# Low half of the expert gates built by ScalarE one token at a time, and the experts' split activations moved in memory

## The chip, the cores and the metric

The kernel runs on one core of a Trainium2 chip. The metric is the time of one execution on the device in microseconds (us), the median of several executions. The engines named below are TensorE (PE, with its weight loads as PEld), VectorE (DVE), ScalarE (ACT), GpSimd (POOL) and SyncE (SP), whose queue issues the DMAs.

## The reference, cut to what matters

Two blocks of two layers each run over 256 tokens of width 1024. The change lies in the expert part of the first block, which runs once in each of its two layers:

```python
N_KEYS, N_EXPERTS, PEER_HEADS, PEER_TOPK = 128, 128 * 128, 8, 16

def peer(xn, w_q, sub_keys, u, v):
    q = (xt @ w_q).astype(float32).reshape(t, PEER_HEADS, 2, PEER_HALF)
    sc = einsum('thpc,pnc->thpn', q, sub_keys)
    top_s, top_i = lax.top_k(sc, PEER_TOPK)
    cand = top_s[:, :, 0, :, None] + top_s[:, :, 1, None, :]
    best_s, best_c = lax.top_k(cand.reshape(t, PEER_HEADS, 256), PEER_TOPK)
    expert = i1 * N_KEYS + i2
    gate = softmax(best_s, axis=-1)
    ...
    act = gelu(einsum('cd,chkd->chk', xc, u[ec]))
    return einsum('chk,chkd->cd', gc * act, v[ec])
```

So each token has 128 pairs of expert and gate, and the result is the sum over those experts of gate times gelu(x·u) times v.

## The kernel before, in words

The kernel computes all 16384 experts densely. `act` holds 128 x 128 x 256 values: for expert 128 n + p the partition is p, the second index n, the third the token. In each layer `peer` goes through three stages.

**Routing** finds the 128 experts and gates of each token, while the first products with u already run (`u_whole`, line 888: one block is 256 experts, two transposes of `raw` into `ut` on VectorE and 16 float32 products of 256 columns on TensorE, which the trace records as 32). At its end `mT`, `nT` and `gp` hold, by partition for the 128 pairs and by column for the 256 tokens, the expert's two indices and the gate, scaled by 32768 and split into a high and a low fp16 half (lines 839 and 840).

**The sweep** (`spread_gates`, line 848) turns this list into a dense gate for every expert. It takes GT = 4 tokens at a time, 64 groups in a layer. For a group VectorE makes `oh` (line 859, where mT equals the index), `eq` (line 861, where nT equals the index) and `rhs` (line 863, eq times the high and the low half of gp, 2 x 128 x 4 values). TensorE multiplies `oh` with `rhs` token by token, high and low half into the same bank of PSUM (line 868, eight products of 128 columns, each with its own weight load). VectorE then multiplies the experts already computed by their gates (line 872) and ScalarE stores the gates of the others (line 874). `oh` has two buffers, `eq` one, `rhs` four. Between the groups stand the blocks of u; after every block come four groups (`SWEEP_STEPS`), and `u_out` (lines 924 to 927) applies gelu and, where gates are there, the gate.

**The v stage** (`v_pair`, line 930) multiplies the 16384 gated values with v. `ah` and `al` are the high and low parts of two slices of `act`; they live in the buffers of `rhs`, and are the stationary operands of 24 products of 512 columns in each of 64 pairs (line 943), so 3072 in two layers. The moving operands are the split rows of v in the ring of weights (`whi`, `wlo`). The last 27 blocks of u run between these pairs with the split scheme (`u_split`, lines 198 to 200 and 906 to 910).

A scheduler puts the instructions of each engine into one fixed order by priorities; `K.ahead()` draws the loads and splits of weights forward, and the products of the gates have a priority of their own (`GPRIO`). Each engine works through its order and waits in place. `raw`, into which the DMAs write, has three buffers.

**Places in memory.** `K.shift` puts an unused tile of so many bytes ahead of a pool's next tiles. In the built program the ring's `whi` and `wlo` begin at multiples of 512 bytes (51200, 55296, 59392, 63488, 67584, 71680). `rhs`, and so `ah` and `al`, begin at 213056, which is 64 bytes past a multiple of 512. The tiles `x`, moving operands of lines 198 to 200, begin 64 bytes below a multiple of 512.

## Time and profile before

| | us |
|---|---|
| median of 3 runs | 3620.2 (3617.34 to 3631.05) |
| profiled execution, its own time | 3630.35 |
| profiled execution, span of its instructions | 3628.6 |
| first sweep, from the first to the last product of gates | 608.6 to 783.9 |
| second sweep | 1926.8 to 2103.6 |
| v stages with the last blocks of u | 783.9 to 1340 and 2103.6 to 2640 |

The granted clock of TensorE over the whole span was 0.975. Busy shares are means over stages with different limits, so the sweep has to be looked at by itself: how long each engine is busy in it, where TensorE stops, and what ends each stop.

### The profile page before, as it was taken

How to read it: one execution, taken by the hardware profiler on the slowest of the kernel's cores; microseconds unless marked ns; L12 is line 12 of the kernel's file. 1: busy time of each engine (PE TensorE's matmuls, PEld its weight loads, DVE VectorE, ACT ScalarE, POOL GpSimd, SP SyncE). 2: the span in 40 equal slices, each digit the busy share in tenths (PEclk: the TensorE clock that was granted, in tenths of full speed). 3: DMA queues.
4: the chain of work that ended last, by engine and by line, in shares of the span. 5: the costliest groups of instructions: out<-in, count | busy, mean ns of one | idle time of the engine just before them, and what ended most of it. 6: DMA issues, size and time to landing. Idle time of an engine off the chain costs nothing. (4 is left out here: it accounts for less than half of the span.)

```text
span 3628.6 us, 60192 instructions
## 1 busy us (share of the span) xinstructions
PE 3484.8 (96%) x23381; PEld 3187.9 (88%) x23381; DVE 2623.3 (72%) x4704; ACT 1475.1 (41%) x2418; POOL 604.2 (17%) x583
## 2 busy tenths in 40 slices
PE   8999998999999999999999999999989999999999
PEld 8898887888888889998888888888789899988999
DVE  6967668876666568775668866666578877698775
ACT  6455111234444446553112144444445344444434
POOL 1200111000000012101120000000033543345441
PEclk9999999999999999999999999999989999999999
DMA  7775756436666567765765346665666534665433
GB/s 178 180 187 140 164 128 139 93 94 189 184 184 187 196 156 173 196 159 147 155 138 113 94 130 190 188 189 186 190 151 141 109 85 116 164 129 120 96 85 126
DMA packets 433976, 541.70 MB, mean 149 GB/s; under 512 B 28665, under 2 KB 392219, under 8 KB 432667
## 3 DMA queue, kind: packets, MB, share of 16 engines
q1 hardware_dynamic: 433690, 537.86, 58.5%
q8 instruction: 183, 3.00, 0.4%
q14 instruction: 103, 0.84, 0.1%
HBM read 530.39 MB, written 6.32 MB: 148 GB/s over the span
## 5 line engine op out<-in xcount | busy, mean ns | idle before, releaser
L170 DVE TENSOR_TENSOR wlo<-raw,whi 128x1024 fp32r<-128x1024 f32 x670 | 862.7, 1293 | 325.8 <-ACT whi L167 311.3
L167 ACT ACTIVATE whi<-raw 128x1024 fp32r<-128x1024 f32 x696 | 728.7, 1051 | 709.0 <-PE mm L199 271.9
L898 PE MATMUL mm<-x,ut 128*128 128x256 f32 x2368 | 542.6, 386 | 1.2 <-ACT act L927 1.2
L200 PE MATMUL mm<-x,wlo 128*128 128x256 f32 x1760 | 506.6, 288 | 14.4 <-DVE wlo L170 14.1
L898 PEld LDWEIGHTS mm<-x,ut 128*128 128x128 f32 x2368 | 453.0, 194 | 64.3 <-ACT act L927 3.9
L198 PE MATMUL mm<-x,whi 128*128 128x256 f32 x1760 | 504.4, 287 | 3.3 <-ACT whi L167 3.3
L199 PE MATMUL mm<-x,whi 128*128 128x256 f32 x1708 | 488.9, 286 | 0.0
L200 PE MATMUL gg<-x,wlo 128*128 128x256 f32 (+1 forms) x1456 | 410.5, 282 | 9.3 <-DVE wlo L170 9.1
L198 PE MATMUL gg<-x,whi 128*128 128x256 f32 (+1 forms) x1456 | 410.9, 282 | 4.9 <-ACT whi L167 4.9
L199 PE MATMUL gg<-x,whi 128*128 128x256 f32 x1400 | 393.6, 281 | 1.3 <-DVE x L303 1.3
L200 PEld LDWEIGHTS mm<-x,wlo 128*128 128x128 f32 x1760 | 340.8, 194 | 18.2 <-DVE wlo L170 17.2
L198 PEld LDWEIGHTS mm<-x,whi 128*128 128x128 f32 x1760 | 340.7, 194 | 10.7 <-issue 5.6
L199 PEld LDWEIGHTS mm<-x,whi 128*128 128x128 f32 x1708 | 331.6, 194 | 1.9 <-issue 0.7
L943 PE MATMUL ax<-wlo,ah 128*128 128x512 f32 x1024 | 323.0, 396 | 2.6 <-DVE wlo L170 2.6
L943 PE MATMUL ax<-whi,al 128*128 128x512 f32 x1024 | 321.4, 395 | 0.0
L200 PEld LDWEIGHTS gg<-x,wlo 128*128 128x128 f32 (+1 forms) x1456 | 276.3, 190 | 11.7 <-DVE wlo L170 11.3
L943 PE MATMUL ax<-whi,ah 128*128 128x512 f32 x1024 | 286.6, 395 | 0.0
L198 PEld LDWEIGHTS gg<-x,whi 128*128 128x128 f32 (+1 forms) x1456 | 275.7, 189 | 8.2 <-ACT whi L167 5.6
L894 DVE STREAM_TRANSPOSE ut<-raw 128x1024 f32<-128x1024 f32 x148 | 181.9, 1236 | 130.8 <-DMA raw<-in_peer_u_dram 114.1
L199 PEld LDWEIGHTS gg<-x,whi 128*128 128x128 f32 x1400 | 265.9, 190 | 3.5 <-DVE x L303 1.4
L943 PEld LDWEIGHTS ax<-wlo,ah 128*128 128x128 f32 x1024 | 190.2, 187 | 54.8 <-DVE wlo L170 9.2
L943 PEld LDWEIGHTS ax<-whi,al 128*128 128x128 f32 x1024 | 191.7, 187 | 47.1
(534 smaller groups left out, 6593.5 us busy)
## 6 DMA issues: line engine op xcount, KB each, us to landing
raw<-in_w_in_dram SPq DMA_DIRECT2D x592, 256.0 KB
raw<-in_peer_u_dram SPq DMA_DIRECT2D x512, 256.0 KB
raw<-in_peer_v_dram SPq DMA_DIRECT2D x128, 1024.0 KB
raw<-in_w_branch_dram SPq DMA_DIRECT2D x16, 1024.0 KB
raw<-in_w_out_dram SPq DMA_DIRECT2D x16, 1024.0 KB
raw<-in_w_peer_q_dram SPq DMA_DIRECT2D x64, 256.0 KB
raw<-in_w_in_dram SPq DMA_DIRECT2D x64, 128.0 KB
raw<-in_w_branch_dram SPq DMA_DIRECT2D x32, 256.0 KB
```

The source lines that it names most:

```text
L167: nc.scalar.activation(view(hi), src, AF.Copy)
L170: (nc.gpsimd if pool else nc.vector).tensor_tensor(view(lo), src, view(hi).bitcast(F32), ALU.subtract)
L198: t.matmul(out, wh, xh, start=start, stop=False)
L199: t.matmul(out, wh, xl, start=False, stop=False)
L200: t.matmul(out, wl, xh, start=False, stop=stop)
L894: nc.vector.transpose(turned[jh], blk)
L898: nc.tensor.matmul(ps[:, jh], turned[jh][:, k].rearrange("p j c -> p (j c)"), xs[:, k], start=k + jh == 0, stop=k == KT - 1 and jh == 1)
L943: nc.tensor.matmul(out[tb][c], lhs[:, j, ts], r[:, c * 512:c * 512 + 512], start=b + j == 0 and lhs is ah and r is vh, stop=b == 63 and j ...
```

## The change

It does three things.

1. `rhs` is made by two engines. VectorE multiplies eq with the high half alone (512 values instead of 1024). The low half is kept in float32 (`gl`), and ScalarE makes its part of `rhs` with four activations a group, one for each token, 128 values each: it reads the token's column of eq, every fourth value, scales it by the column of `gl`, one value for each partition, and writes one run of 128 values.
2. The products of line 868 stand in two lines, 871 (high) and 872 (low); the low one now reads its moving operand as one run and not every fourth value.
3. `SHIFTS["peer"]` goes from 64 to 0 bytes in both layers. `gp` shrinks by 512 bytes and `gl` adds 1024, so that `rhs`, `ah` and `al` begin at 213504 instead of 213056 in the built program: a multiple of 512 bytes, as the ring's tiles do.

```diff
--- before.py
+++ after.py
@@ -33,7 +33,7 @@
 
 
 URGENT = 3000
-SHIFTS = {"zp": (0, 288), "zp2": (384, 384), "ple": (384, 128), "peer": (64, 64)}
+SHIFTS = {"zp": (0, 288), "zp2": (384, 384), "ple": (384, 128), "peer": (0, 0)}
 SQ_ACT = (2, 5, 7)
 HPOOL = ()
 WPOOL = 0
@@ -73,6 +73,7 @@
         self.consts()
 
     def shift(self, pool, size, name="shift"):
+
 
         if size:
             pool.tile([128, size // 4], F32, name=name, bufs=1)
@@ -719,7 +720,8 @@
     nc.vector.tensor_copy(io4, io[:, :, None].to_broadcast([128, 128, GT]))
     mT = pool.tile([128, S], FP16, name="mT")
     nT = pool.tile([128, S], FP16, name="nT")
-    gp = pool.tile([128, 2, S], FP16, name="gp")
+    gp = pool.tile([128, S], FP16, name="gp")
+    gl = pool.tile([128, S], F32, name="gl")
     sc_b = [scratch([128, 4, 128]) for _ in range(2)]
     qs_b = [scratch([128, 2, S]) for _ in range(2)]
     cand_b = [scratch([128, 2, NCAND]) for _ in range(2)]
@@ -836,9 +838,8 @@
                 nc.scalar.activation(dst, ps[:, 0:S], AF.Copy)
             else:
                 rest = m_f.rearrange("p b n -> p (b n)")
-                nc.scalar.activation(gp[:, 0], ps[:, 0:S], AF.Copy, scale=GSCALE)
-                nc.vector.scalar_tensor_tensor(gp[:, 1], ps[:, 0:S], GSCALE, gp[:, 0], op0=ALU.mult,
-                                               op1=ALU.subtract)
+                nc.scalar.activation(gp, ps[:, 0:S], AF.Copy, scale=GSCALE)
+                nc.vector.scalar_tensor_tensor(gl, ps[:, 0:S], GSCALE, gp, op0=ALU.mult, op1=ALU.subtract)
             yield
 
     made, spread = [0], [0]
@@ -859,14 +860,16 @@
             nc.vector.tensor_tensor(oh, io4, tok(mT), ALU.is_equal)
             eq = pool.tile([128, 128, GT], FP16, name="eq", tag="eq", bufs=1)
             nc.vector.tensor_tensor(eq, io4, tok(nT), ALU.is_equal)
-            rhs = pool.tile([128, 2, 128, GT], FP16, name="rhs", tag="rhs", bufs=4)
-            nc.vector.tensor_tensor(rhs, eq[:, None].to_broadcast([128, 2, 128, GT]),
-                                    gp[:, :, None, ts].to_broadcast([128, 2, 128, GT]), ALU.mult)
+            rhs = pool.tile([128, 2, 128 * GT], FP16, name="rhs", tag="rhs", bufs=4)
+            hi = rhs[:, 0].rearrange("p (n t) -> p n t", t=GT)
+            lo = rhs[:, 1].rearrange("p (t n) -> p t n", t=GT)
+            nc.vector.tensor_tensor(hi, eq, tok(gp), ALU.mult)
+            for t in range(GT):
+                nc.scalar.activation(lo[:, t], eq[:, :, t], AF.Copy, scale=gl[:, t0 + t:t0 + t + 1])
             with tc.high_priority(offset=GPRIO):
                 for t in range(GT):
-                    for part in range(2):
-                        nc.tensor.matmul(pg[:, t], oh[:, :, t], rhs[:, part, :, t], start=t + part == 0,
-                                         stop=t == GT - 1 and part == 1)
+                    nc.tensor.matmul(pg[:, t], oh[:, :, t], hi[:, :, t], start=t == 0, stop=False)
+                    nc.tensor.matmul(pg[:, t], oh[:, :, t], lo[:, t], start=False, stop=t == GT - 1)
             pg = pg.rearrange("p t n -> p n t")
             n = made[0]
             nc.vector.scalar_tensor_tensor(act[:, :n, ts], act[:, :n, ts], 1.0 / GSCALE, pg[:, :n],
```

The order of the instructions moves in the two sweeps; outside them VectorE, ScalarE and TensorE keep theirs but for a few neighbours, and the order of the DMAs is the same. Four places follow, all in the first layer. The number behind a name tells one tile from another of that name; `eq_5872` is the first group's.

VectorE at the opening of the sweep, before:

```order
L861 TENSOR_TENSOR eq_5872<-io4_4654,nT_4657 128x512
L840 SCALAR_TENSOR_TENSOR gp_4658<-ax_5810,gp_4658 128x256
L863 TENSOR_TENSOR rhs_5874<-eq_5872,gp_4658 128x1024
L861 TENSOR_TENSOR eq_5889<-io4_4654,nT_4657 128x512
L863 TENSOR_TENSOR rhs_5891<-eq_5889,gp_4658 128x1024
L894 STREAM_TRANSPOSE ut_6233<-raw_6228 128x1024
L861 TENSOR_TENSOR eq_5906<-io4_4654,nT_4657 128x512
L863 TENSOR_TENSOR rhs_5908<-eq_5906,gp_4658 128x1024
L861 TENSOR_TENSOR eq_5923<-io4_4654,nT_4657 128x512
L863 TENSOR_TENSOR rhs_5925<-eq_5923,gp_4658 128x1024
L894 STREAM_TRANSPOSE ut_6235<-raw_6228 128x1024
```

and after:

```order
L862 TENSOR_TENSOR eq_5872<-io4_4653,nT_4656 128x512
L842 SCALAR_TENSOR_TENSOR gl_4658<-ax_5810,gp_4657 128x256
L866 TENSOR_TENSOR rhs_5874<-eq_5872,gp_4657 128x512
L862 TENSOR_TENSOR eq_5893<-io4_4653,nT_4656 128x512
L897 STREAM_TRANSPOSE ut_6297<-raw_6292 128x1024
L866 TENSOR_TENSOR rhs_5895<-eq_5893,gp_4657 128x512
L862 TENSOR_TENSOR eq_5914<-io4_4653,nT_4656 128x512
L866 TENSOR_TENSOR rhs_5916<-eq_5914,gp_4657 128x512
L875 SCALAR_TENSOR_TENSOR act_4651<-act_4651,gg_5869 128x38x4
L860 TENSOR_TENSOR oh_5912<-io4_4653,mT_4655 128x512
L862 TENSOR_TENSOR eq_5935<-io4_4653,nT_4656 128x512
```

The product for `rhs` has half the values, a transpose now stands between the second `eq` and its product, and the third and fourth group's work begins after the first group's gates are used (line 875, before 872).

ScalarE at the same place, before (834 to 839 make mT, nT and gp; 874 stores gates; 924 and 927 are gelu):

```order
L839 ACTIVATE gp_4658<-ax_5810 128x256
L924 ACTIVATE mm_5946<-mm_5946 128x2x32
L874 ACTIVATE act_4651<-gg_5869 128x90x4
L874 ACTIVATE act_4651<-ax_5886 128x90x4
L874 ACTIVATE act_4651<-ax_5903 128x90x4
L874 ACTIVATE act_4651<-gg_5920 128x90x4
L927 ACTIVATE act_4651<-mm_5851 128x2x240
```

and after:

```order
L841 ACTIVATE gp_4657<-ax_5810 128x256
L868 ACTIVATE rhs_5874<-eq_5872,gl_4658 128x128 x4
L868 ACTIVATE rhs_5895<-eq_5893,gl_4658 128x128 x4
L868 ACTIVATE rhs_5916<-eq_5914,gl_4658 128x128 x4
L877 ACTIVATE act_4651<-gg_5869 128x90x4
L927 ACTIVATE mm_5962<-mm_5962 128x2x32
L868 ACTIVATE rhs_5937<-eq_5935,gl_4658 128x128 x4
L877 ACTIVATE act_4651<-ax_5890 128x90x4
L877 ACTIVATE act_4651<-ax_5911 128x90x4
```

Four activations for each group now stand between the stores, in one queue with them.

VectorE in the settled part of the sweep, before (925 multiplies a block of u by its gates):

```order
L925 TENSOR_TENSOR act_4651<-mm_6431,act_4651 128x2x112
L861 TENSOR_TENSOR eq_6602<-io4_4654,nT_4657 128x512
L894 STREAM_TRANSPOSE ut_6817<-raw_6810 128x1024
L859 TENSOR_TENSOR oh_6600<-io4_4654,mT_4656 128x512
L863 TENSOR_TENSOR rhs_6604<-eq_6602,gp_4658 128x1024
L872 SCALAR_TENSOR_TENSOR act_4651<-act_4651,ax_6548 128x52x4
L872 SCALAR_TENSOR_TENSOR act_4651<-act_4651,ax_6565 128x52x4
L872 SCALAR_TENSOR_TENSOR act_4651<-act_4651,gg_6582 128x52x4
L859 TENSOR_TENSOR oh_6646<-io4_4654,mT_4656 128x512
L861 TENSOR_TENSOR eq_6648<-io4_4654,nT_4657 128x512
L863 TENSOR_TENSOR rhs_6650<-eq_6648,gp_4658 128x1024
```

and after:

```order
L862 TENSOR_TENSOR eq_6705<-io4_4653,nT_4656 128x512
L928 TENSOR_TENSOR act_4651<-mm_6527,act_4651 128x2x112
L866 TENSOR_TENSOR rhs_6707<-eq_6705,gp_4657 128x512
L897 STREAM_TRANSPOSE ut_6977<-raw_6970 128x1024
L860 TENSOR_TENSOR oh_6703<-io4_4653,mT_4655 128x512
L862 TENSOR_TENSOR eq_6726<-io4_4653,nT_4656 128x512
L860 TENSOR_TENSOR oh_6724<-io4_4653,mT_4655 128x512
L875 SCALAR_TENSOR_TENSOR act_4651<-act_4651,ax_6660 128x52x4
L875 SCALAR_TENSOR_TENSOR act_4651<-act_4651,ax_6681 128x52x4
L866 TENSOR_TENSOR rhs_6728<-eq_6726,gp_4657 128x512
L862 TENSOR_TENSOR eq_6776<-io4_4653,nT_4656 128x512
L866 TENSOR_TENSOR rhs_6778<-eq_6776,gp_4657 128x512
```

Each transpose, product and `oh` has another place between the `eq`s; in the kernel before VectorE alone read `eq`.

VectorE near the end of the sweep, where the first transposes for `u_split` are drawn forward, before (line 906):

```order
L863 TENSOR_TENSOR rhs_7186<-eq_7184,gp_4658 128x1024
L861 TENSOR_TENSOR eq_7230<-io4_4654,nT_4657 128x512
L906 STREAM_TRANSPOSE raw_7524<-raw_7524 128x8x4x32 x2
L863 TENSOR_TENSOR rhs_7232<-eq_7230,gp_4658 128x1024
L894 STREAM_TRANSPOSE ut_7425<-raw_7420 128x1024
L872 SCALAR_TENSOR_TENSOR act_4651<-act_4651,gg_7164 128x64x4
L859 TENSOR_TENSOR oh_7228<-io4_4654,mT_4656 128x512
```

and after (line 909):

```order
L866 TENSOR_TENSOR rhs_7456<-eq_7454,gp_4657 128x512
L897 STREAM_TRANSPOSE ut_7681<-raw_7676 128x1024
L862 TENSOR_TENSOR eq_7475<-io4_4653,nT_4656 128x512
L909 STREAM_TRANSPOSE raw_7780<-raw_7780 128x8x4x32 x2
L866 TENSOR_TENSOR rhs_7477<-eq_7475,gp_4657 128x512
L875 SCALAR_TENSOR_TENSOR act_4651<-act_4651,gg_7380 128x64x4
L860 TENSOR_TENSOR oh_7452<-io4_4653,mT_4655 128x512
```

Behind the drawn-forward transposes stood a product for `rhs`, a transpose of 1024 values and line 872 ahead of the next `oh`; now only a product of half the size and line 875.

## Rows read from the trace of the kernel before

**Rows 1.** Page, part 1: busy time, share and instructions of each engine.
```profile
PE 3484.8 (96%) x23381; PEld 3187.9 (88%) x23381; DVE 2623.3 (72%) x4704; ACT 1475.1 (41%) x2418; POOL 604.2 (17%) x583
```

**Rows 2.** Windows; columns: length, busy PE, PEld, DVE, ACT, POOL, clock, DMA.
```profile
608.60:783.90 175.30, 168.61 (x984) 148.54 (x983) 143.84 (x293) 38.04 (x95) 0.00 (x0) 0.96 0.37 87
1926.80:2103.60 176.80, 169.35 (x984) 149.13 (x983) 143.69 (x293) 37.95 (x95) 0.00 (x0) 0.95 0.37 87
...
608.60:619.60 11.00, 9.09 (x56) 7.37 (x55) 10.79 (x27) 3.50 (x8) 0.00 (x0) 0.72 0.65 140
...
640.00:694.00 54.00, 54.00 (x326) 48.49 (x326) 46.04 (x96) 12.19 (x31) 0.00 (x0) 1.00 0.44 98
```

**Rows 3.** Timeline of TensorE's weight loads, 655 to 680; columns: start, length, instruction.
```profile
657.10 1.97 PEld L868 LDWEIGHTS <-oh 128*128 128x128 f16 x16
...
662.25 5.50 PEld L898 LDWEIGHTS mm<-x,ut 128*128 128x128 f32 x26
667.78 1.97 PEld L868 LDWEIGHTS <-oh 128*128 128x128 f16 x16
```

**Rows 4.** Groups by line on VectorE, whole span; columns: busy us, mean ns, idle before.
```profile
L863 DVE TENSOR_TENSOR rhs<-eq,gp 128x1024 f16<-128x1024 f16 x128 | 87.3, 682 | 2.1
L861 DVE TENSOR_TENSOR eq<-io,nT 128x512 f16<-128x512 f16 x128 | 53.0, 414 | 1.6
...
L894 DVE STREAM_TRANSPOSE ut<-raw 128x1024 f32<-128x1024 f32 x148 | 181.9, 1236 | 130.8 <-DMA raw<-in_peer_u_dram 114.1 <-PE mm L898 16.2
...
L872 DVE SCALAR_TENSOR_TENSOR act<-act,ax 128x240 f32<-128x240 f32 x6 | 2.4, 400 | 1.6 <-PE ax L868 1.6
```

**Rows 5.** Groups by line on ScalarE: an activation of 128 values.
```profile
L1467 ACT ACTIVATE ddh<-packed,gt 128x128 fp32r<-128x128 f32 x64 | 20.2, 390 | 18.2 <-PE ax L1473 11.8 <-DVE gt L1281 3.9 <-POOL S L1587 2.5
```

**Rows 6.** Timeline, first sweep: VectorE's first `eq`, then TensorE; idle before in brackets.
```profile
604.38 0.41 DVE L861 TENSOR_TENSOR eq<-io,nT 128x512 f16<-128x512 f16 x1
...
612.16 1.11 PE L868 MATMUL ax<-rhs,oh 128*128 128x128 f16 x8 [1.53 <-DVE oh L859]
...
615.71 1.11 PE L868 MATMUL ax<-rhs,oh 128*128 128x128 f16 x8 [0.39 <-DVE rhs L863]
616.75 6.31 PE L898 MATMUL mm<-x,ut 128*128 128x256 f32 x20
...
629.25 2.99 PE L898 MATMUL mm<-x,ut 128*128 128x256 f32 x13
...
704.06 2.06 PE L868 MATMUL ax<-rhs,oh 128*128 128x128 f16 x16 [0.65 <-DVE oh L859]
```

**Rows 7.** Timeline of VectorE and TensorE, first sweep, where line 906 is reached.
```profile
755.90 2.37 DVE L906 STREAM_TRANSPOSE raw<-raw 128x1024 f32<-128x1024 f32 x2 [3.13 <-DMA raw<-in_peer_u_dram]
...
760.69 1.11 PE L868 MATMUL ax<-rhs,oh 128*128 128x128 f16 x8 [1.97 <-DVE oh L859]
...
763.42 1.11 PE L868 MATMUL gg<-rhs,oh 128*128 128x128 f16 x8 [1.62 <-DVE rhs L863]
```

**Rows 8.** Line 868's weight loads: ns least/median/most, first and last start.
```profile
L868 PEld LDWEIGHTS <-oh x1024: 111/117/136, 608.4 to 2103.2; 128*128 128x128 f16 x171
```

**Rows 9.** Timeline of TensorE in three places: start, length, instruction.
```profile
259.06 0.28 PE L199 MATMUL gg<-x,whi 128*128 128x256 f32 x1
...
260.20 0.28 PE L200 MATMUL gg<-x,wlo 128*128 128x256 f32 x1
...
887.24 0.63 PE L943 MATMUL ax<-wlo,ah 128*128 128x512 f32 x2
887.71 0.63 PE L943 MATMUL ax<-whi,al 128*128 128x512 f32 x2
888.17 0.28 PE L198 MATMUL gg<-x,whi 128*128 128x256 f32 x1
...
1340.53 0.28 PE L198 MATMUL ax<-x,whi 128*128 128x256 f32 x1
...
1342.33 0.28 PE L198 MATMUL ax<-x,whi 128*128 128x256 f32 x1
```

## The prediction

> **What bounds the kernel now.** The page comes first: TensorE is busy 96% of the span, VectorE 72%, ScalarE 41% [rows 1]. That is a mean, so next comes the table by windows for the two sweeps, the only places where instructions change [rows 2]. They last 175.30 and 176.80 us, with TensorE busy 168.61 and 169.35, VectorE 143.84 and 143.69, ScalarE 38.04 and 37.95. The line to look at is the settled stretch from 640 to 694: TensorE is busy 54.00 of 54.00 us there, VectorE 46.04, and ScalarE 12.19, all at full clock. So VectorE does not set the pace in the settled sweep, though it is close.
>
> The timeline of the weight loads gives TensorE's block [rows 3]: from one pair of groups at 657.10 to the one a block later at 667.78 are 10.68 us. Sixteen loads for gates take 1.97 (0.123 each), 26 for u 5.50 (0.2115 each). A sweep has 984 products [rows 2], 512 of gates and so 472 of u: 512 x 0.123 + 472 x 0.2115 = 162.8 us. So the sweeps lose 175.3 - 162.8 = 12.5 and 176.8 - 162.8 = 14.0 us, and 26.5 us in all is the most that a quicker VectorE could give back if TensorE's products cost the same. [...]
>
> **Part by part: VectorE and ScalarE in the settled sweep.** The product for `rhs` falls from 1024 to 512 values. The new one has the kinds and size of `eq`'s row: 0.414 for 0.682, 0.268 us x 128 groups = 34.3 us less on VectorE [rows 4]. ScalarE gets 512 activations of 128 values with a scale from a tile. Line 1467 is the nearest row: the same size and such a scale, 0.390 each on average, and 20.2 us for 64, so 0.316 apiece where they overlap [rows 5]. I take both: four in a row are 0.39 + 3 x 0.316 = 1.34 us. For a block of four groups ScalarE goes from 12.19 / 54 x 10.68 = 2.4 us to 2.4 + 16 x 0.316 = 7.5 (8.6 at 0.390), under 10.68. VectorE goes from 46.04 / 54 x 10.68 = 9.1 to 8.0. TensorE stays the longest: both edits cost and gain nothing here.
>
> The new wait is that `eq` has one buffer and ScalarE now reads it too. The next `eq` waits for four activations, 1.34 us and a handoff, some 1.45, and behind it in VectorE's queue stand `oh` and the transposes, for which TensorE waits. In the settled order the shortest work between two `eq` is an `oh`, two of line 875 and a product: 0.41 + 0.40 + 0.40 + 0.41 = 1.62 (`oh` and the product by the row of `eq`) [rows 4]. That covers it with little to spare; without the cover the excess would stand once or twice in a block. ScalarE's queue is the other place: the activations stand behind stores that wait for VectorE. Laid end to end, the low half is ready some 3 us before its product in a settled block. Satisfied waits of the products I take at nothing: the 16 loads in 1.97 already span two waits.
>
> **The opening.** Here VectorE is late already, and the wait bites. Laid end to end with the durations above from the first `eq` at 604.38 [rows 6]: `gl` ends at 605.2, the four activations at 606.5, the second `eq` at 607.0, a transpose and the product at 608.6, the third `eq` at 609.0, its activations at 610.4, the fourth `eq` and a transpose at 612.1, line 875, `oh` and the product at 613.1. Two groups later the sixth's product is ready at 616.6; before, the sixth group's products run from 615.71 [rows 6], so 0.9 us are lost. Then three `eq` follow each other with one product between (1.85 us a group for 1.1), and the order gives TensorE 12 groups and 31 products of u up to a point that it now reaches with 10 groups and 31 products at 629.25 [rows 6]. Two groups more would be 631.2 in the kernel before; I get 632 to 634. I take +1.5 a sweep, from -1 (clock regained) to +5 (0.39 for each activation).
>
> **Line 906 and the middle.** The DMA that VectorE waits for at line 906 is issued when a transpose releases a buffer of `raw`. Between the two the order had a product of line 925, two `rhs`, two `oh`, two `eq` and two of line 872; now it has two `oh`, three `eq`, two products, two of line 875 and a transpose. That is 1.24 + 0.41 for a transpose and an `eq`, less 2 x 0.27 and less line 925, about half a us: 0.6 more, so the wait of 3.13 becomes some 2.5 [rows 7]. But behind it stand 0.41 + 0.40 + 0.41 = 1.2 us to the end of the next `oh` instead of 0.68 + 1.24 + 0.40 + 0.41 = 2.7: the stop of 1.97 falls to about 0.5, that of 1.62 mostly goes, and some clock with it. I take -3 a sweep, from 0 to -6. The middle stop has the same kind: -1, from 0 to -2.
>
> **The low half in one run.** Line 868's loads take 117 at the median and 111 at the least [rows 8]. If half the products no longer disturb the next load, 512 x 0.006 = 3.1 us are won, at worst nothing; I take -1.5. [...]
>
> **Where the split activations lie.** This has by far the widest bounds. Lines 198 to 200 show that a place can matter: where the moving tile lies 64 bytes below a multiple of 512 and the weights on one, the products follow each other at 0.114 us (10 steps from 259.06 to 260.20); in the `ple` stage, where the two lie alike modulo 512, at 0.120 (15 steps from 1340.53 to 1342.33) [rows 9]. For line 943 the distance is now 64 as well and becomes 0. Its products follow each other at 0.235 (two from 887.24 to 887.71). The pair from 887.71 to 888.17 is the nearest row to the new state: its second product runs while weights of line 198 are loaded, which lie on a multiple of 512 as its moving operand does, and the step is no longer: 0.23 [rows 9]. So I take 0. The ends are one such difference a product, 0.114 x 2 = 0.228 against 0.120 x 2 = 0.240: 0.0067 us either way of what it takes now, x 3072 = 20.5 us less or more. [...]
>
> **Sum.** 2 x (1.5 - 3 - 1) - 1.5 + 0 = -6.5 us on the profiled execution's 3630.35, its span 3628.6 and 1.75 around it: 3623.9. That execution was 10.2 above the median of the runs, so against 3620.2 the forecast is 3614, no change that can be told: a measurement of this kernel tells about 0.5%, here 18 us. Its own range is 3602 to 3626.
>
> **The rivals.** *The place pays*: line 943 gets the better pace. For it speaks that lines 198 to 200 have two paces, against it the pair at 887.71. It gives 3614 - 20.5 = 3593, chance 17%. The reverse, the worse pace, gives 3634, within the 0.5%, chance 8%.
> *VectorE was the bound after all*: all of the sweeps' stops and the clock lost with them go. Then 26.5 us are won, 3594. Against it speak the 54.00 of 54.00; chance 6%.
> *ScalarE becomes the bound (slower)*: place, its queue in the sweep. It decides from (10.68 - 2.4) / 16 = 0.52 us an activation; at 0.60, should reading every fourth value cost so much, a block lasts 2.4 + 9.6 = 12.0, and 32 blocks cost 42 us more: 3656. Against it: line 1467's 0.390. Chance 12%, with lesser forms in which the wait for `eq` recurs in each block.
> *The change does little of what it says* (the run of the low half and the place move nothing) lies inside the forecast.
>
> **How the numbers follow.** Forecast 57%, place better 17%, place worse 8%, VectorE bound 6%, ScalarE bound 12%. Faster by over 0.5% (under 3602): 17 + 6 and 2 from the forecast's edge = 25%. Slower by over 0.5% (above 3638): 12%. Within: 63%. The range from 3592 to 3638 holds all but ScalarE's case and some of the far ends.
>
> **What would show it.** Right: in 640 to 694's counterpart TensorE still without a gap, VectorE at some 75%, ScalarE at some 70%; the product for `rhs` at 0.41, the activations at 0.32 to 0.39; a later sixth group at the opening; smaller stops behind line 909; line 946 (943 before) at 0.233 a product. Wrong: VectorE waiting for ScalarE ahead of `eq` in every block, products of line 872 waiting for ScalarE, or another pace of line 946, which is the first thing to look at, since there 3072 products multiply every nanosecond.

## The result, and the profile after

The changed kernel takes **3585.07 us** (median of 4 runs, 3573.58 to 3587.82), the kernel before, on the same chip, 3624.15 (median of 4). The ratio is **0.9886, 95% interval 0.9855 to 0.9917**: some 30 to 53 us less. The forecast was 3614 us, with a range from 3592 to 3638, and most of the chance on "no change that can be told". So it was wrong: the change is faster, and by more than the range allows. The profiled execution of after took 3587.82 us, its span 3586.1.

Part 1 of the page of after (busy time, share, instructions), which answers to [rows 1]:

```profile
PE 3441.6 (96%) x23381; PEld 3169.8 (88%) x23381; DVE 2589.4 (72%) x4704; ACT 1629.2 (45%) x2930; POOL 606.3 (17%) x583
```

TensorE's busy time fell by 43 us, VectorE's by 34, and ScalarE's rose by 154. So the engine that was called the bound has less to do; the prediction had allowed 1.5 us for that. The windows of after, which answer to [rows 2] (length, busy PE, PEld, DVE, ACT, POOL, clock, DMA share, GB/s):

```profile
599.00:760.30 161.30, 153.97 (x988) 137.01 (x987) 128.57 (x296) 112.73 (x344) 0.00 (x0) 0.97 0.41 96
1900.90:2062.70 161.80, 154.73 (x988) 137.52 (x987) 128.45 (x295) 112.72 (x344) 0.00 (x0) 0.96 0.41 96
...
640.00:694.00 54.00, 54.00 (x346) 48.55 (x345) 45.28 (x105) 38.51 (x120) 0.00 (x0) 1.00 0.51 114
```

The two sweeps last 161.30 and 161.80 us in place of 175.30 and 176.80: 29 us less. In the settled stretch TensorE is still busy for 54.00 of 54.00 us, now with 346 products in place of 326. It is still the bound, and its products have become cheaper. The timeline of TensorE in the settled sweep of after shows which (start, length, instruction; line 871 is the high product of a token, line 872 the low one):

```profile
655.30 0.28 PE L871 MATMUL ax<-rhs,oh 128*128 128x128 f16 x1
655.40 0.24 PE L872 MATMUL ax<-rhs,oh 128*128 128x128 f16 x1
655.48 0.28 PE L871 MATMUL ax<-rhs,oh 128*128 128x128 f16 x1
```

From 655.30 to 655.48 is one token, both halves. Over all pairs that follow each other the median is 175 ns; before it was 236, since every product started 118 ns after the one ahead of it. Read the starts, not the lengths: the lengths (0.28 and 0.24) overlap.

The second place where time went is the stage of v. Line 943 is now line 946, and its products of 512 columns follow each other at a median of 227 ns, before at 233. From the start of its first product to the start of its last a stage took 519.2 and 518.6 us before, and takes 511.5 and 515.9 after.

The rest of the two profiled executions differs in both directions though the program is the same there. Over the 14 traces of this case the first product of the gates starts between 598.8 and 608.6 us (before: the last of them), and the part behind the second stage of v lasts between 992.6 and 1008.1. Much of that is chance between executions: in two traces of the changed kernel the last part alone took 1006.0 and 993.8. Whether any of it belongs to the change is not shown, and nothing below is taken from it. Everything below is read from the sweeps and the stages of v, and the times of runs stand beside it.

### The profile page after: what moved, and what is told of

Its sections match the earlier page's. It is cut to its first block, busy times and chain, and to the rows that moved or that the text cites. A ratio compares the mean times of both kernels' runs of the same rounds, so it can differ in the third digit from the quotient of the medians.

```text
span 3586.1 us, 60820 instructions
## 1 busy us (share of the span) xinstructions
PE 3441.6 (96%) x23381; PEld 3169.8 (88%) x23381; DVE 2589.4 (72%) x4704; ACT 1629.2 (45%) x2930; POOL 606.3 (17%) x583
```

## The experiments

**What each theory says.** *The run* (the low half of a token lying in one piece): a product whose moving operand takes every fourth value costs TensorE about 118 ns, one whose operand lies in one run about half of that; this made the sweeps shorter. *The place*: the sweeps and the stage of v gained from the new place. *VectorE*: its relief (34 us less work) made the sweeps shorter. The first three experiments separate the three parts of the change, and in each the sweeps and the stages of v are read apart.

| kernel | time us (median) | before us, same chip | ratio, 95% interval | sweeps us | stages of v us |
|---|---|---|---|---|---|
| before | | | | 175.0, 176.5 | 519.2, 518.6 |
| after | 3585.07 | 3624.15 | 0.9855 to 0.9917 | 160.9, 161.6 | 511.5, 515.9 |
| run and ScalarE, old place | 3587.69 | 3618.13 | 0.9894 to 0.9931 | 160.6, 161.7 | 517.7, 518.0 |
| place alone | 3607.46 | 3618.13 | 0.9961 to 0.9996 | 175.4, 175.3 | 513.5, 512.7 |
| place and ScalarE, no run | 3596.18 | 3618.13 | 0.9919 to 0.9957 | 172.6, 171.7 | 512.7, 513.2 |
| high half in one run too (permuted write) | 3764.11 | 3618.13 | 1.0376 to 1.0413 | 251.6, 254.7 | 504.9, 512.6 |
| both in one run, VectorE by token | 3660.16 | 3616.60 | 1.0095 to 1.0137 | 197.1, 197.5 | 513.3, 512.8 |
| both in one run, low from high | 3586.38 | 3616.60 | 0.9891 to 0.9930 | 162.4, 162.3 | 513.9, 513.3 |
| low half every second value | 3581.26 (1 run) | 3616.60 | | 162.8, 162.0 | 512.6, 514.2 |
| both halves every eighth value | 3774.18 (1 run) | 3616.60 | | 260.2, 259.5 | 512.3, 511.5 |
| high half every second value | 3560.29 | 3631.28 | 0.9794 to 0.9836 | 151.4, 151.3 | 512.8, 514.7 |
| after, again | 3580.83 | 3631.28 | 0.9848 to 0.9883 | 162.2, 161.4 | 513.0, 513.1 |
| after, split activations at 256 and 128 | 3584.19 (1 run) | 3631.28 | | 162.2, 161.0 | 514.6, 518.0 |
| after, split activations at 32 and 448 | 3585.78 (1 run) | 3631.28 | | 161.0, 161.7 | 516.3, 517.0 |

Sweeps and stages are taken from the first start of their products to the last (first layer, second layer), in one trace of each kernel. The same kernel traced twice (after) differs by up to 1.2 us in a sweep and 2.8 in a stage of v.

**1. The run and ScalarE without the place.** The changed kernel, with the pool shifted back by 64 bytes:

```
-SHIFTS = {..., "peer": (0, 0)}
+SHIFTS = {..., "peer": (64, 64)}
```

> The changed kernel with the split activations back at 64 bytes above a multiple of 512 (the place of before); the low half in one run and its making by ScalarE stay. Theory (the run): a product whose moving operand takes every fourth value costs TensorE about 118 ns, one whose operand lies in one run about 57, so a pair of products for a token takes 175 ns in place of 236 whatever the place; the sweeps last about 161 us each as after the change, and the 512-column products of v go back to 233 ns from 227: the time is 3585 to 3598 us. Rival (the place): the sweeps' gain came from the new place of the moving operands, which rhs shares; then they go back to 175 and 176.5 us and the time to 3612 to 3625. Rival (VectorE): its relief gave the gain; this run has it too and can't tell it from the run.

Windows of the two sweeps and the timeline of line 946:

```profile
601.60:762.50 160.90, 153.71 (x988) 136.62 (x987) 128.48 (x296) 112.63 (x344) 0.00 (x0) 0.97 0.41 96
1902.80:2064.80 162.00, 154.96 (x988) 137.41 (x987) 128.56 (x296) 112.80 (x344) 0.00 (x0) 0.96 0.41 95
```

```profile
1201.52 0.63 PE L946 MATMUL ax<-wlo,ah 128*128 128x512 f32 x2
1201.99 0.63 PE L946 MATMUL ax<-whi,al 128*128 128x512 f32 x2
1202.45 0.63 PE L946 MATMUL ax<-wlo,ah 128*128 128x512 f32 x2
```

Four products from 1201.52 to 1202.45: 0.2325 each (median 233 ns). The sweeps keep all of their gain at the old place, the stages of v lose theirs. So the place has no part in the sweeps.

**2. The place alone.** The kernel before, with the shift taken out:

```
-SHIFTS = {..., "peer": (64, 64)}
+SHIFTS = {..., "peer": (0, 0)}
```

> The kernel before with the pool's shift of 64 bytes taken out in both layers, so that rhs and the split activations lie on a multiple of 512 as after the change; nothing else. Theory (the run): the sweeps stay at 175 to 177 us; only the 512-column products of v go from 233 to 227 ns, of which the two stages of v show some 3 to 8 us each: the time is 3610 to 3617 us. Rival (the place): the sweeps fall to 161 us as well and the time to 3585 to 3595. Rival (place is nothing): 233 ns and 3620 to 3625.

The same two views:

```profile
606.10:781.80 175.70, 169.09 (x984) 148.97 (x983) 143.90 (x293) 38.04 (x95) 0.00 (x0) 0.96 0.37 87
1916.90:2092.60 175.70, 168.96 (x984) 148.94 (x983) 143.77 (x293) 37.96 (x95) 0.00 (x0) 0.96 0.37 87
```

```profile
1200.32 0.62 PE L943 MATMUL ax<-wlo,ah 128*128 128x512 f32 x2
1200.77 0.61 PE L943 MATMUL ax<-whi,al 128*128 128x512 f32 x2
1201.22 0.62 PE L943 MATMUL ax<-wlo,ah 128*128 128x512 f32 x2
```

Four products from 1200.32 to 1201.22: 0.225 (median 227). The sweeps stay, the stages of v lose 5.7 and 5.9 us, and the time 10.7 by the medians (1.4 to 14 by the interval). So the place is worth some 11 us, all of it in the stage of v.

It could have been 3072 x 0.006 = 18. Part of the rest goes to VectorE. TensorE's waits in the first stage of v (window 790 to 1300), of weight loads and of products, in the kernel before and in this one (engine, line, releaser: us in all, times, longest):

```profile
PEld ax L943 <- DVE wlo L170: 5.3, 10, 1.1
...
PE ax L943 <- DVE wlo L170: 1.7, 3, 0.7
```

```profile
PEld ax L943 <- DVE wlo L170: 8.1, 10, 1.4
...
PE ax L943 <- DVE wlo L170: 3.5, 6, 1.0
```

The faster products wait longer for the low half of the weights, which VectorE makes. With 1536 x 0.006 = 9.2 us to be had in a stage, these rows account for some 2 to 3 of the 3.5 that did not arrive (they overlap, so they are not added). That was read, not tested.

**3. Place and ScalarE without the run.** The changed kernel, low half laid out as before:

```
-            lo = rhs[:, 1].rearrange("p (t n) -> p t n", t=GT)
+            lo = rhs[:, 1].rearrange("p (n t) -> p n t", t=GT)
...
-                nc.scalar.activation(lo[:, t], eq[:, :, t], AF.Copy, scale=...)
+                nc.scalar.activation(lo[:, :, t], eq[:, :, t], AF.Copy, scale=...)
...
-    nc.tensor.matmul(pg[:, t], oh[:, :, t], lo[:, t], start=False, stop=t == GT - 1)
+    nc.tensor.matmul(pg[:, t], oh[:, :, t], lo[:, :, t], start=False, stop=t == GT - 1)
```

> The changed kernel with the low half laid out as before (four tokens interleaved, every fourth value a token's), still made by ScalarE token by token, still at the new place. Theory (the run): the pair of products goes back to 236 ns and the sweeps to 172 to 177 us, though VectorE is as relieved as after the change: 3608 to 3618 us. Rival (VectorE was the bound): the sweeps stay near 161 us, 3585 to 3592. Rival (ScalarE's strided writes cost more): activations well above 0.39 us each and sweeps above 177.

Windows, timeline of the settled sweep, and ScalarE's group of the low half (busy us, mean ns, idle before):

```profile
598.80:771.70 172.90, 167.75 (x988) 149.39 (x987) 129.33 (x296) 122.69 (x345) 0.00 (x0) 0.97 0.38 89
1906.90:2078.80 171.90, 166.66 (x988) 148.68 (x987) 129.10 (x296) 122.36 (x345) 0.00 (x0) 0.97 0.38 90
```

```profile
658.25 0.30 PE L871 MATMUL ax<-rhs,oh 128*128 128x128 f16 x1
658.37 0.30 PE L872 MATMUL ax<-rhs,oh 128*128 128x128 f16 x1
658.49 0.30 PE L871 MATMUL ax<-rhs,oh 128*128 128x128 f16 x1
```

```profile
L868 ACT ACTIVATE rhs<-eq,gl 128x128 f16<-128x128 f16 x512 | 191.3, 565 | 80.6 <-DVE eq L862 73.8 <-DVE gl L842 4.7 <-PE ax L871 1.5
```

The pair is back at 236 ns (658.25 to 658.49) and the sweeps at 172.6 and 171.7. VectorE is as relieved here as after the change (129 us in a sweep), so its relief is worth 2.8 and 3.7 us a sweep against the place alone, and the run 11.6 and 10.1 more. The time came out lower than I expected of it, since my expectation of 3608 to 3618 left these 6 us out; the sweeps are what separates the theories. ScalarE's activations take 565 ns here for 400 after (means), so writing every fourth value costs them; TensorE is busy for 53.94 of 54 us from 620 to 674 all the same, and in the first sweep none of its stops, here or after, ends with a low half. So what the run gave came from TensorE's own steps.

**4 to 6. The high half in one run as well.** If the run is the cause, it can be had a second time. First by VectorE's same product, written permuted:

```
-            hi = rhs[:, 0].rearrange("p (n t) -> p n t", t=GT)
-            nc.vector.tensor_tensor(hi, eq, tok(gp), ALU.mult)
+            hi = rhs[:, 0].rearrange("p (t n) -> p t n", t=GT)
+            nc.vector.tensor_tensor(hi.rearrange("p t n -> p n t"), eq, tok(gp), ALU.mult)
...
```

> The changed kernel with the high half in one run too: VectorE's product reads as before and writes it permuted. Theory (the run): both products of a token cost about 57 ns, the pair 115 in place of 175, 256 pairs a sweep: TensorE's share of a sweep falls by another 15 us, to sweeps of 146 us and a time near 3556, if VectorE's permuted write costs no more than now. If VectorE's write in runs of one value costs more (above 0.6 us for a product of 0.41), VectorE sets the pace of a sweep and it ends between 150 and 165 us, 3565 to 3592. Rival (VectorE was the bound, the run nothing): the sweeps stay at 161 or get longer.

VectorE's group of the product, and the settled window:

```profile
L866 DVE TENSOR_TENSOR rhs<-eq,gp 128x512 f16<-128x512 f16 x128 | 312.3, 2440 | 1.7
```

```profile
640.00:690.00 50.00, 36.78 (x204) 30.29 (x202) 49.17 (x61) 23.64 (x72) 0.00 (x0) 0.77 0.27 60
```

The pair is 112 ns at the median, so each product costs 56 in one run. But VectorE's product takes 2.44 us where it took 0.42, VectorE is busy for 49.17 of 50, and the sweeps last 252 us. I had bounded that cost far too low. The rival with VectorE as the bound is real, only not in the kernel that was changed. Next with VectorE's writes in a row, one instruction a token and half:

```
-            nc.vector.tensor_tensor(eq, io4, tok(nT), ALU.is_equal)
-            nc.vector.tensor_tensor(hi, eq, tok(gp), ALU.mult)
...
-                nc.scalar.activation(lo[:, t], eq[:, :, t], AF.Copy, scale=...)
+                nc.vector.tensor_scalar(hi[:, t], io1, nf[:, at], gf[:, at], op0=ALU.is_equal, op1=ALU.mult)
+                nc.vector.tensor_scalar(lo[:, t], io1, nf[:, at], gl[:, at], op0=ALU.is_equal, op1=ALU.mult)
...
```

> The changed kernel with both halves in one run each, made by VectorE token by token (column number equal to nT, times the gate's half: one instruction of 128 values with two scalars from a tile); eq, its product and ScalarE's four activations are gone, and VectorE's writes lie in a row. Theory (the run): both products of a token cost 57 ns, the pair 115 in place of 175, so TensorE's share of a sweep falls by 256 x 0.060 = 15 us against the changed kernel; of the 15.6 us that the low half's run saved on TensorE in the same way, about 11 reached the sweep's length, so the sweeps end at 146 to 151 us and the time at 3560 to 3570 us, if eight such instructions take VectorE no longer than the eq and the product did (0.83 us a group, so 0.10 each). Rival (VectorE becomes the bound): at 0.20 each VectorE gets 0.8 us a group more, a block of four groups takes it 8.0 + 3.1 = 11.1 us, longer than TensorE's 8.2, and the sweeps last 175 us or more: 3612.

```profile
L875 DVE TENSOR_SCALAR rhs<-io,nf,gl x512: 261/305/338, 598.6 to 2127.3; 128x128 f16<-128x128 f16 x171
```

```profile
640.00:690.00 50.00, 40.15 (x263) 34.38 (x261) 50.00 (x183) 9.90 (x25) 0.00 (x0) 0.93 0.37 85
```

The pair is 112 ns again, but each instruction takes 0.305 us at the median, eight of them 2.4 us a group: VectorE is busy for 50.00 of 50. The rival's price (0.20) was still too low. Then the low half by ScalarE from the high half, which leaves VectorE four:

```
+                nc.vector.tensor_scalar(hi[:, t], io1, nf[:, at], gf[:, at], op0=ALU.is_equal, op1=ALU.mult)
+                nc.scalar.activation(lo[:, t], hi[:, t], AF.Copy, scale=gr[:, at])
...
```

> As the kernel with both halves in one run made by VectorE, but the low half is made by ScalarE from the high half (times the quotient of the two gates), so VectorE has four instructions of 128 values in place of eq and its product, and ScalarE the four activations that it has now, which read in one run. Theory (the run): pair of products 115 ns, sweeps 146 to 151 us, 3560 to 3570 us, and here VectorE gains as well, so the same or a little better than with VectorE alone. Rival (ScalarE sets the pace): with a block at some 8.2 us ScalarE's 2.4 + 16 x 0.33 = 7.7 leaves little cover and the products wait for its activations: sweeps of 155 to 160 us, 3575 to 3585.

```profile
640.00:690.00 50.00, 46.15 (x334) 40.60 (x333) 44.88 (x138) 35.59 (x113) 0.00 (x0) 1.00 0.47 108
```

The window is the settled one. No better than after: 162.4 us a sweep. TensorE's products are cheaper by 16 us a sweep, and it idles for them: 46.15 of 50 us busy, its stops ended by an activation of u (2.1 us) and by `oh` on VectorE (1.7). Four instructions at 0.306 make 1.22 us, where `eq` and the product take 0.83. The gain went into waits for the engines that feed TensorE.

**7 and 8. What the distance of the values costs.** The low half with every second value, and both halves with every eighth:

```
-            lo = rhs[:, 1].rearrange("p (t n) -> p t n", t=GT)
+            lo = rhs[:, 1].rearrange("p (h n t) -> p h n t", h=2, t=2)
...
```

```
-            rhs = pool.tile([128, 2, 128 * GT], FP16, name="rhs", tag="rhs", bufs=4)
+            rhs = pool.tile([128, 128, 2 * GT], FP16, name="rhs", tag="rhs", bufs=4)
+            hi = rhs[:, :, 0:GT]
+            lo = rhs[:, :, GT:]
...
```

> The changed kernel with the low half laid out two tokens interleaved (every second value a token's) in place of one run. It measures the low product's step by the distance of its values. If the step follows the bytes that are passed over, it is 57 ns at every value, 118 at every fourth, and near 57 to 80 at every second; if any gap costs the same, it is 118 and the sweeps go back to 172 us; if only a gap of more than 4 bytes costs, it stays at 57 and the sweeps at 161. The time follows: 3585 to 3600 us.

> The changed kernel with both halves of four tokens interleaved: every eighth value is a token's (16 bytes apart), for the high and the low product alike. If the step doubles with the distance (57 ns at one, 118 at four), both products take some 236 ns, and a sweep gets 512 x 0.118 = 60 us longer than the 172 us with every fourth: 230 us, 3705 in all. If it has levelled off at 118 ns by every fourth value, the sweeps stay near 172 us and the time near 3596.

Timelines of the settled sweep, every second value first:

```profile
655.34 0.28 PE L871 MATMUL ax<-rhs,oh 128*128 128x128 f16 x1
655.43 0.24 PE L872 MATMUL ax<-rhs,oh 128*128 128x128 f16 x1
655.52 0.28 PE L871 MATMUL ax<-rhs,oh 128*128 128x128 f16 x1
```

```profile
661.30 0.41 PE L872 MATMUL ax<-rhs,oh 128*128 128x128 f16 x1
661.53 0.41 PE L871 MATMUL ax<-rhs,oh 128*128 128x128 f16 x1
661.76 0.41 PE L872 MATMUL ax<-rhs,oh 128*128 128x128 f16 x1
```

With every second value the pair is 180 ns at the median, so the low product takes 180 - 118 = 62. With every eighth each product takes 230. So 128 values of 2 bytes cost 56 ns in a row, 62 at a distance of 4 bytes, 118 at 8, and 230 at 16. From 4 bytes on the cost goes with the bytes passed over; "levelled off" and "any gap costs the same" both fall. The sweeps with every eighth value are 31 us longer than their products make them (172 + 512 x 0.112 = 229 us, measured 260). The window of the first sweep shows TensorE busy nearly throughout, and a granted clock of 0.81. A second window, with two products of gates in it, has a granted clock of 0.50:

```profile
603.50:864.00 260.50, 257.45 (x988) 176.61 (x987) 134.05 (x294) 191.00 (x345) 0.00 (x0) 0.81 0.25 58
...
630.60:640.60 10.00, 10.00 (x40) 6.15 (x39) 6.54 (x18) 9.11 (x18) 0.00 (x0) 0.50 0.47 105
```

```profile
634.72 0.41 PE L872 MATMUL ax<-rhs,oh 128*128 128x128 f16 x1
634.95 0.41 PE L871 MATMUL ax<-rhs,oh 128*128 128x128 f16 x1
```

That is where the 31 us are: the products of u follow each other at 216 ns where the granted clock is 1.00 and at 427 where it is 0.50, and take 141 us of this sweep for 108 in experiment 3. The products of gates keep their 230 ns at 0.50 (634.72 to 634.95), as those with every fourth value in the kernel before keep 118 (its granted clock was 0.50 from 614 to 620), while products in a row go from 56 to 107 in experiment 4, whose granted clock was 0.77 from 640 to 690. So at 8 and at 16 bytes the price did not follow the granted clock. What paces these products is not shown.

**9. Every second value for the high half.** From these prices comes a version that leaves VectorE's work as it is: `eq` and the high half two tokens interleaved in place of four, low half in one run by ScalarE.

```
-            eq = pool.tile([128, 128, GT], FP16, name="eq", tag="eq", bufs=1)
-            nc.vector.tensor_tensor(eq, io4, tok(nT), ALU.is_equal)
+            eq = pool.tile([128, 2, 128, 2], FP16, name="eq", tag="eq", bufs=1)
+            two = lambda x: x[:, ts].rearrange("p (h t) -> p h t", t=2)[:, :, None, :].to_broadcast([128, 2, 128, 2])
+            nc.vector.tensor_tensor(eq, io2[:, None].to_broadcast([128, 2, 128, 2]), two(nT), ALU.is_equal)
...
-            hi = rhs[:, 0].rearrange("p (n t) -> p n t", t=GT)
+            hi = rhs[:, 0].rearrange("p (h n t) -> p h n t", h=2, t=2)
-            nc.vector.tensor_tensor(hi, eq, tok(gp), ALU.mult)
+            nc.vector.tensor_tensor(hi, eq, two(gp), ALU.mult)
...
```

> The changed kernel with eq and the high half laid out two tokens interleaved (every second value a token's) in place of four; low half in one run by ScalarE as now, same place. A product with every second value was measured at 62 ns (pair of 180 less 118), one in a run at 56: the pair becomes some 118 in place of 175, TensorE's share of a sweep 256 x 0.057 = 14.6 us less. Theory (the run, TensorE still the bound): if VectorE's eq and product keep their 0.41 us with runs of two values, its block of four groups stays at 8.0 us against TensorE's 8.3, and half to all of the 14.6 us reach the sweep: 148 to 154 us, 3560 to 3575 us, faster than both kernels. Rival (VectorE pays for the shorter runs): at 0.7 us each VectorE's block is 10.4 us and the sweeps last 165 us or more: 3590 or more.

> The changed kernel once more, beside the others on the same chip: 3575 to 3590 us, sweeps of 161 us, 512-column products at 227 ns.

VectorE's groups, the windows, and the timeline of the settled sweep (line 874 is the high product, 875 the low one):

```profile
L869 DVE TENSOR_TENSOR rhs<-eq,gp 128x512 f16<-128x512 f16 x128 | 53.8, 420 | 2.2
L865 DVE TENSOR_TENSOR eq<-io,nT 128x512 f16<-128x512 f16 x128 | 52.8, 412 | 18.0 <-ACT rhs L871 15.4
```

```profile
601.40:753.10 151.70, 141.65 (x988) 123.31 (x987) 127.13 (x296) 109.91 (x344) 0.00 (x0) 0.95 0.44 102
1888.20:2039.80 151.60, 141.58 (x988) 123.30 (x987) 127.20 (x296) 109.99 (x344) 0.00 (x0) 0.95 0.44 102
...
640.00:690.00 50.00, 49.59 (x351) 43.78 (x350) 45.10 (x105) 37.79 (x122) 0.00 (x0) 1.00 0.53 118
```

```profile
657.60 0.22 PE L874 MATMUL gg<-rhs,oh 128*128 128x128 f16 x1
657.66 0.22 PE L875 MATMUL gg<-rhs,oh 128*128 128x128 f16 x1
657.72 0.22 PE L874 MATMUL gg<-rhs,oh 128*128 128x128 f16 x1
```

The pair takes 115 ns, VectorE's two instructions 0.41 and 0.42 us as before, and a sweep 151.4 and 151.3 us. At 3560.29 us against 3580.83 for the changed kernel on the same chip (0.9794 to 0.9836 against 0.9848 to 0.9883 of the kernel before) it beats both. TensorE is busy for 49.59 of 50 us and a pair is within 3 ns of two products in a row (112), so little is left to win here this way.

**10 and 11. Other places.** The split activations 256, 128, 32 and 448 bytes above a multiple of 512, one place a layer: `"peer": (256, 128)` and `"peer": (32, 448)` in the changed kernel.

> The changed kernel with the split activations 256 bytes above a multiple of 512 in the first layer and 128 in the second. Known: 227 ns a 512-column product at 0, 233 at 64. If only the same place modulo 512 gives the better pace, both stages of v show 233; if the pace grows with the distance, 256 shows the most; if what counts is 64 above alone, both show 227.

> The changed kernel with the split activations 32 bytes above a multiple of 512 in the first layer and 448 (64 below the next) in the second. If only the same place gives the better pace, both stages of v show 233; if 64 bytes make the step, the first shows 227 and the second 233; if above and below differ, the two stages differ.

Timelines of line 946 at 32 above (first layer) and at 448 (second layer):

```profile
1200.52 0.63 PE L946 MATMUL ax<-wlo,ah 128*128 128x512 f32 x2
...
1201.45 0.63 PE L946 MATMUL ax<-wlo,ah 128*128 128x512 f32 x2
...
2480.88 0.62 PE L946 MATMUL ax<-wlo,ah 128*128 128x512 f32 x2
...
2481.80 0.62 PE L946 MATMUL ax<-wlo,ah 128*128 128x512 f32 x2
```

The medians are 227 ns at 0 and at 256, 233 at 32 and at 64, 232 at 128, 229 at 448. By whole stages 448 stands with the slow places (517.0 us, with 518.0 at 128 and 516.3 at 32, for 514.6 at 256). None of the rules that I had written down fits all of them. Lines 198 to 200 had their slower pace, 0.120 us, where the two operands lie alike modulo 512 [rows 9], line 946 has its better one, 227 ns, there, so "alike" is no rule either. The pace is a matter of the place, two places share the best one, and why stays open. The two times, 3584.19 and 3585.78 us, are those of the changed kernel within what single runs tell.

## Why the prediction was wrong

**What the change gave, part by part.** ScalarE's share and VectorE's relief: 2.8 + 3.7 us (experiment 3 against 2). The run: 11.6 + 10.1 (after against experiment 3). The place: 5.7 + 5.9 (experiment 2 against before). The sum is 39.8 us, the difference of the medians 39.1; with single traces that differ by 1 to 3 us from each other, so close a fit is partly luck. The prediction had 5, 1.5 and 0 for them.

**That TensorE is the bound in the settled sweep was right,** with 54.00 of 54.00 us before and after. The bound on the gain carried a condition, "if TensorE's products cost the same", and this is the step that failed: the change made half of the gates' products cheaper. The floor of 162.8 us and the 26.5 us above it were worked out from 0.123 us a weight load [rows 3]. But each load there is followed by its product, and in the kernel before both follow each other at a median of 118 ns, so the loads' interval does not say which of the two sets it. The sweeps went below that floor to 160.9 and 161.6. (The 0.123 and 0.2115 are lengths of merged rows divided by their counts; start to start it is 0.118 and 0.216, and the two errors nearly cancel: 162.4.)

**The low half in one run was mis-sized:** -1.5 us, 3.1 at most, where 21.7 were measured. The bound came from 117 against 111 ns, the median and the least of one form of load [rows 8]. Every load there stood before a product with every fourth value, so the least of them says nothing of a product in one run, and no row of before held one. An end of the range was missing: the nearest row for a product of 128 columns in one run would have been half of the 0.114 that a product of 256 columns takes [rows 9], that is 0.057 by estimate; it measured 0.056. The gain on TensorE is 256 x 0.061 = 15.6 us a sweep, of which some 11 arrive. In the first sweep TensorE's four largest stops are 1.60, 1.08, 1.17 and 1.19 us in experiment 3 and 1.92, 1.08, 1.91 and 1.68 after; the faster products wait longer for VectorE and ScalarE.

With every fourth value a product of 128 columns takes 118 ns, with every second 62, in a row 56, each in a stream with its weight loads. A price at twice that of a row is to be explained before it is called a floor.

**The place: taken at 0, measured at 11.6.** The rival *the place pays* (17%) had its mechanism and its place right, with 20.5 us, of which 3072 x 0.006 = 18 are in TensorE's steps. The row that decided against it, the pair from 887.71 to 888.17 [rows 9], was no row of the new state. By the trace its two steps are 233 ns each, like those ahead of it. In the kernel before, the 54 last products of line 943 ahead of a block of lines 198 to 200, beside which weights on a multiple of 512 are loaded, take 233 ns at the median; with the place alone changed (experiment 2), where the same weights are loaded beside them, 226. So the load that runs beside a product did not bring the better pace; what moved, and the pace with it, is the place of the product's own stationary operand, and no row of line 943 had that at another place. With that the 0 was a guess. (The ends were not even either: 0.235 - 0.228 = 0.007 down and 0.240 - 0.235 = 0.005 up are 21.5 and 15.4 us, not 20.5 both ways.)

**VectorE's relief: about right.** The sum was 1.5 - 3 - 1 = -2.5 us a sweep, measured -2.8 and -3.7. By steps, against the place alone: the 41st product of the gates comes 1.2 us later after the first (8.4 and 8.3 us for 7.1), as the opening was said to, and by the 121st 1.2 and 0.2 of that are regained. From the 121st to the 401st 0.7 are won (the middle, where [rows 6] has the stop of 0.65 us at 704.06; said to be 1). From there to the end 2.1 and 4.0 (line 906, said to be 3). VectorE waits 1.52 us for the DMA there in experiment 3 in place of 3.13 [rows 7], and TensorE's two stops behind it are 1.17 and 1.19 in place of 1.97 and 1.62 (about 0.5, and mostly gone, were said). In the changed kernel itself the products come up to that place earlier, and the stops are back. The timeline of all engines around it:

```profile
734.62 2.37 PE L901 MATMUL mm<-x,ut 128*128 128x256 f32 x10
735.50 2.37 DVE L909 STREAM_TRANSPOSE raw<-raw 128x1024 f32<-128x1024 f32 x2 [1.83 <-issue]
...
738.90 0.29 PE L871 MATMUL ax<-rhs,oh 128*128 128x128 f16 x1 [1.91 <-DVE oh L860]
...
742.15 1.22 PE L901 MATMUL mm<-x,ut 128*128 128x256 f32 x2 [1.68 <-ACT act L930]
```

Line 909 still holds VectorE, `oh` stands behind it, and TensorE stops 1.91 us for `oh`, then 1.68 for an activation. So the two stops only shrank in experiment 3 and did not go in the changed kernel: that step was wrong in its mechanism, and that the sum came out about right is partly luck.

**ScalarE: right.** The low half's group in after, with VectorE's product and `eq` (busy us, mean ns, idle before):

```profile
L866 DVE TENSOR_TENSOR rhs<-eq,gp 128x512 f16<-128x512 f16 x128 | 53.7, 420 | 2.2
L862 DVE TENSOR_TENSOR eq<-io,nT 128x512 f16<-128x512 f16 x128 | 52.7, 412 | 18.3 <-ACT rhs L868 16.0
```

The product takes 0.42 (0.41 was said), ScalarE is busy for 38.51 of 54 us (71%, some 70 was said), its activations take 0.397 at the median. VectorE is busy for 45.28 of 54 us, 84% where some 75 was said: its work shrank as forecast (in experiment 3 it is 41.02 of 54, 76%), but TensorE's products became cheaper, so more of VectorE's work falls into the same stretch. VectorE waits 16.0 us in all for the low half ahead of `eq`, in both sweeps, off TensorE's path in the settled stretch. The rival *ScalarE becomes the bound* needed 0.52 an activation beside TensorE's old block, and did not come; *VectorE was the bound after all* gave the right size of the sweeps' gain for the wrong reason, and experiment 3 shows it worth 6.5 us.

## What to carry to other kernels

A busy TensorE says that it is the bound, not that its products are as cheap as they can be (54.00 of 54.00 us here, with pairs of 236 ns and of 175): compare the start-to-start interval of a product with that of the same number of columns read in a row, and look at the layout of the moving operand where they differ. When a layout has to be traded between engines, price each writer by a run first: here every second value gave TensorE nearly all (a pair of 115 ns, for 112 in a row) and cost VectorE nothing (0.42 us a product, as in the changed kernel), while a full permutation cost VectorE six times that (2.44). And a floor worked out from one operand's interval in a stream of pairs bounds nothing until the other operand has been changed: here the floor was 162.8 us, and the sweeps went to 160.9.

## What the runs showed of the hardware

- A product's price went with the layout of its moving operand: 128 fp16 values took TensorE 56 ns in a row, 62 (59 to 62, in two kernels) at 4 bytes, 118 at 8, 230 at 16. Where the granted clock was 0.50 the 118 (the kernel before) and the 230 (experiment 9) stayed; in experiment 4, with a granted clock of 0.77 from 640 to 690, the 56 became 107. The stationary operand `oh` lies at 8 bytes in all of these kernels, and its loads kept up with 56 ns a product.
- VectorE's product of 512 values took 0.42 us in runs of four values and in runs of two, and 2.44 us where each value went to another run. An instruction of 128 values with two scalars from a tile took 0.305.
- ScalarE's activation of 128 values took 0.400 us written in a row, 0.431 at every second value, 0.565 at every fourth and 1.02 at every eighth (means).
- The place of a 512-column product's stationary operand (0 to 448 bytes above a multiple of 512, the moving one always on a multiple) moved its pace between 227 and 233 ns, by no rule that four more places showed. The weights loaded beside the product, on a multiple of 512, did not bring the better pace (233 ns).
